# Hybrid decoder trunk: twelve unit pairs a layer by seven products, weight sums built in scratch memory by accumulating transfers

## The chip, the cores and the metric

One core of one Trainium2 chip runs the whole program. The metric is device time in microseconds (us) of one execution, the median of several. A profiled execution gives the trace that is read below; the trace's span runs from the first instruction to the last, and the execution's own time is a little longer than its span.

The core has a matrix engine (PE in the profile, with its weight loads as PEld), a vector engine (DVE), a scalar engine (ACT), a general engine (POOL), and a queue that issues transfers (SP). POOL can issue transfers too. Each engine works through its own list of instructions in order and waits at an instruction until what it needs is there.

## The reference, cut to what matters

Two layers, each on 512 tokens of width 1024:

```
h    = rmsnorm(x) ; proj = h @ w_in            # q,k,v,z,b,a | q,k,v | gate A, gate B
y_a  = deltanet(...) @ w_up_dn                 # gated delta rule, 8 heads of 128
y_b  = sliding_window_attention(...) @ w_up_sw # 16 query heads, window 128
mix  = (sigmoid(gA) * y_a + sigmoid(gB) * y_b) @ w_o
x    = x + rmsnorm(mix)
ff   = square(relu(rmsnorm(x) @ w_ff1)) @ w_ff2   # 1024 -> 4096 -> 1024
x    = x + rmsnorm(ff)
```

Everything is float32. The kernel keeps that precision by splitting each operand into a rounded part and a remainder and by summing three products (high x high, high x low, low x high), so one product of two blocks is three matmuls.

## The kernel before, in words

**Weights.** All weight chunks lie packed in one input, `wpk`, 128 partitions by 1024 numbers each (512 KB). `load` brings one chunk into a buffer `wr` (six of them, `WR`); `prefetch` rounds it on ACT into `wh` (line 384) and takes the remainder on DVE into `wl` (line 385); `weights()` hands out the next chunk and keeps four split chunks ahead (`LOOK`). The list `specs` fixes the order of chunks for the whole program, and each of its entries is a chunk to load or a small function that makes one.

**A layer in order.** The B projections; then the attention loop of 16 rounds, in which each round computes one or more input-projection units (`MIX`: K for DeltaNet keys, G and A for gates) and one group of sliding-window attention (`att_group`); then branch B's up projection (eight `ps_us` units); then the DeltaNet heads; then branch A's up projection (`ps_ud`), the output projection (`ps_wo`) and the MLP.

In a round of the attention loop the second half of a group masks the transposed probabilities on POOL (two selects `pc`, line 1017, one for the rounded part and one for the remainder) and PE multiplies them with the values (`ps_o`, line 1023). POOL also computes the powers `irk` (line 829) and the rotary products `rt` (lines 911 to 916). SP moves each head's decay matrix `D`, keys `kkd` and matrix `ud` to and from scratch memory; DVE uses `D` at line 837.

**The MLP.** The hidden width of 4096 is cut into four groups `s` of eight units of 128 columns. A single unit is `mm_a`: 8 blocks of the contraction times three matmuls, each 128 by 128 by 512 columns. Two neighbouring units may instead be computed together, as a 2 by 2 block product by seven half-size products (a Strassen-Winograd form): `ff1` calls `mm_h` seven times, each 4 blocks times three matmuls of 256 columns. The operands of these products on the side of the weights are sums of the two units' halves; those on the side of the tokens (`n1` to `n4`) are made once a layer by `combos`. `SEQ` says which units of a group go singly and which as a pair; before the change group 0 has only singles, group 1 two pairs, group 2 three, group 3 four: nine pairs a layer.

The sums of a pair's weights are made by `up_specs`/`one`: it loads both units into two `wr` buffers and adds their halves on DVE into two more (line 343, four additions of 128 by 512 a pair). A pair then uses three and a half chunks: the first unit, sum a, sum b, and the second half of the second unit.

Groups 0 to 2 multiply the result with `w_ff2` by seven products again (`mm_c`: P1 to P7, two chunks each, 24 matmuls of 512 columns a product). Their left operands are made by `lefts` after every second pair (or fourth unit), P1 among them. The last product of a group, P4 (`fourth`), is split in two and its second half put into the next group's first pair when that group begins with a pair.

**What sets the order.** The code is traced in program order, then a scheduler with a model of durations places each instruction in its engine's list. Where the code opens an `Order`, the traced order of the named engines is kept; `keep_in_program_order` pins a single instruction. A transfer issued by SP waits in SP's list until the buffers it needs are free, and everything behind it in that list waits with it.

Of the kernel before, what the change touches and what calls it, by code (L numbers as in the profile page):

```python
# [20 lines left out]
P = 128  # L21
# [20 lines left out]
WR = 6  # L42
FF_ORDER = (0, 4, 1, 5, 2, 6, 3, 7)
XB = 6
SEQ = (FF_ORDER, (0, 1, (4, 5), (2, 3), 6, 7), ((0, 1), (4, 5), (2, 3), 6, 7), ((0, 1), (2, 3), (4, 5), (6, 7)))
# [82 lines left out]
def hybrid_trunk(ctx, tc, x, positions, pre_mix_g, dn_conv_w, dn_a_log, dn_dt_bias, dn_norm_g,  # L128
# [193 lines left out]
    def up_specs(l, s):  # L322
# [4 lines left out]
        def unit(m):  # L327
            return load(("w_ff1", l, 0, (s * 8 + m) * P, 0))

        def one(ms):  # L330
            b = {}

            def raw():
                b["0"], b["1"] = (unit(m) for m in ms)
                return b["0"]

            def of(n_):
                b[n_] = wp.tile([P, 1024], F32, name="wr", bufs=WR)
                x0, x1, x2, x3 = b["0"][:, :512], b["0"][:, 512:], b["1"][:, :512], b["1"][:, 512:]
                yb = b["a"][:, 512:]  # L340
                for o_, i0, i1 in (((b[n_][:, :512], x0, x2), (yb, b[n_][:, :512], x3)) if n_ == "a" else
                                   ((b[n_][:, 512:], x2, x3), (b[n_][:, :512], yb, x1))):
                    tt(out=o_, in0=i0, in1=i1, op=ALU.add)  # L343
                return b[n_]

            return raw, lambda: of("a"), lambda: of("b"), lambda: b["1"][:, 512:]
# [13 lines left out]
        return out + [(last, -1)] * bool(last)  # L360

# [243 lines left out]
    for l in range(depth):  # L605
# [437 lines left out]
        late, klate = (), []  # L1043
        for i in range(16):
            us = []
# [249 lines left out]
        for m in range(KT):  # L1295
# [5 lines left out]
            steps(2 if m < 6 else 40)  # L1301
            if m == 1:
                turn0()
# [66 lines left out]
        mm_b4(pss, mT)  # L1370
        m0, s0 = [], []
# [93 lines left out]
        def ff1(done, rest=None):  # L1465
# [4 lines left out]
            for n, e in enumerate(SEQ[s]):  # L1470
                if not isinstance(e, tuple):
# [35 lines left out]
                mm_h(y, c2, 4, ops["n2"], False)  # L1507
# [5 lines left out]
                mm_h(z, c2, 0, ops["n1"], False)  # L1513
# [18 lines left out]
        for s in range(3):  # L1532
# [9 lines left out]
            def lefts(X, Y):  # L1542

                a11, a21, a12, a22 = X[:, 0:512], X[:, 512:1024], Y[:, 0:512], Y[:, 512:1024]
                make("P1", T[5], a11)
# [17 lines left out]
            def done(ms, ps):  # L1563
# [130 lines left out]
```

## Time and profile before

| | us |
|---|---|
| median of 3 runs (1818.12 to 1818.74) | 1818.7 |
| the profiled execution's own time | 1816.19 |
| its span | 1814.5 |
| PE busy in the span | 1794.6 |
| DVE busy | 1375.1 |
| ACT busy | 1007.5 |
| POOL busy | 210.6 |

The granted TensorE clock was 0.999 over the span. The transfer engines were busy for 49.2% of the span with SP's queue and 0.0% with POOL's.

How to read it: a group of instructions is given as line, engine, operation, output<-input, shapes, count, busy time and mean duration in ns. A matmul's duration is longer than the distance to the next one, since matmuls are pipelined; what a matmul costs PE is the distance between starts, which the rows in order of time show. In those rows the first column is the start in us from the span's start, the second the duration in us, and a bracket at the end tells how long the engine had been idle and what released it. `x2` at the end of a row means two such instructions, merged.

### The profile page before, as it was taken

Reading aid. Unit: us, or ns where it says so; the run is one execution under the profiler, and the core shown is the slowest. Engines: PE = TensorE matmul, PEld = TensorE weight load, DVE = VectorE, ACT = ScalarE, POOL = GpSimd, SP = SyncE. Lnnn points to the kernel's source line nnn. Section 1 sums busy time; section 2 is a strip of 40 time slices with the busy share of each in tenths; the row PEclk is TensorE's granted clock in tenths of the full one; section 3 lists DMA queues with packets and bytes.
Section 4 is the critical chain, followed back from the end, with each engine's and each line's share of the span. In section 5 each row is a group of like instructions: output and inputs, shape, how many; then the busy total and the mean of one; then the engine's idle time right before and its main releaser. Section 6 shows DMA issues by size and latency. Waiting matters only on the chain.

```text
span 1814.5 us, 28394 instructions
## 1 busy us (share of the span) xinstructions
PE 1794.6 (99%) x10252; PEld 1524.7 (84%) x10252; DVE 1375.1 (76%) x2590; ACT 1007.5 (56%) x2065; POOL 210.6 (12%) x386
## 2 busy tenths in 40 slices
PE   9999999999999999999999999999999999999998
PEld 8878878888788888989898887888877888889896
DVE  5499796887666878898556997968875669698973
ACT  6678742444434656566556877234443347566572
POOL 0322102221101000000013221022111010000000
PEclk9999999999999999999999999999999999999999
DMA  5633447655463254554445334585545533555551
GB/s 201 203 112 121 111 146 226 178 172 152 117 208 129 82 164 156 174 180 145 168 160 176 106 127 111 169 232 159 163 140 154 171 116 105 174 162 164 174 178 56
DMA packets 146431, 278.60 MB, mean 154 GB/s; under 512 B 33569, under 2 KB 66657, under 8 KB 146290
## 3 DMA queue, kind: packets, MB, share of 16 engines
q1 hardware_dynamic: 145778, 276.75, 49.2%
q8 instruction: 81, 1.33, 0.3%
q14 instruction: 60, 0.49, 0.1%
q0 software_dynamic: 512, 0.03, 0.0%
HBM read 239.38 MB, written 37.36 MB: 153 GB/s over the span
## 4 chain that ended last, share of the span: by engine, by line
PE 88%; DVE 4%; ACT 4%; DMA 2%; issue 1%; POOL 0%; SPq 0%; DVEq 0%; POOLq 0%; ACTq 0%
PE ps_b L459 3%; PE ps_b L461 3%; PE ps_b L463 3%; PE ps_f L400 2%; PE ps_f L401 2%; PE ps_f L402 2%; PE ps_us L400 2%; PE ps_ud L400 2%; PE ps_us L401 2%; PE ps_ud L401 2%; PE ps_ud L402 2%; PE ps_us L402 2%; PE ps_vp L400 2%; PE ps_vp L402 2%; PE ps_vp L401 1%; PE ps_qp L401 1%
## 5 line engine op out<-in xcount | busy, mean ns | idle before, releaser
L384 ACT CAST wh<-wr 128x1024 fp32r<-128x1024 f32 (+2 forms) x368 | 372.7, 1019 | 430.4 <-PE ps_us L401 60.2
L385 DVE TENSOR_TENSOR wl<-wr,wh 128x1024 fp32r<-128x1024 f32 (+2 forms) x368 | 434.9, 1189 | 183.8 <-ACT wh L384 180.2
L526 POOL TENSOR_TENSOR pr<-pq,pw 128x1 f32<-128x1 f32 x16 | 9.8, 615 | 790.1 <-DVE pq L525 790.1
L459 PE MATMUL ps_b<-wh,h_h 128*128 128x432 f32 (+1 forms) x192 | 71.1, 370 | 0.0
L461 PE MATMUL ps_b<-wl,h_h 128*128 128x432 f32 (+1 forms) x192 | 70.4, 367 | 0.0
L463 PE MATMUL ps_b<-wh,h_l 128*128 128x432 f32 (+1 forms) x192 | 70.3, 366 | 0.0
L400 PE MATMUL ps_f<-g_h,wh 128*128 128x512 f32 x160 | 62.4, 390 | 0.0
L401 PE MATMUL ps_f<-g_l,wh 128*128 128x512 f32 x160 | 62.4, 390 | 0.0
L402 PE MATMUL ps_f<-g_h,wl 128*128 128x512 f32 x160 | 62.2, 389 | 0.0
L401 PE MATMUL ps_qp<-h_l,wh 128*128 128x512 f32 x128 | 53.9, 421 | 0.0
L400 PE MATMUL ps_vp<-h_h,wh 128*128 128x512 f32 x128 | 53.7, 420 | 0.0
L402 PE MATMUL ps_vp<-h_h,wl 128*128 128x512 f32 x128 | 53.7, 419 | 0.0
L995 ACT ACTIVATE M<-M,nm 128x128 f32<-128x128 f32 x128 | 49.8, 391 | 5.9 <-DVE nm L990 5.8
L400 PE MATMUL ps_qp<-h_h,wh 128*128 128x512 f32 x128 | 51.8, 405 | 0.0
L343 DVE TENSOR_TENSOR wr<-wr 128x512 f32<-128x512 f32 x72 | 47.5, 685 | 5.5 <-DMA wr<-in_weights_dram 5.2
L400 PE MATMUL ps_kp<-h_h,wh 128*128 128x512 f32 x128 | 51.6, 403 | 0.0
L402 PE MATMUL ps_qp<-h_h,wl 128*128 128x512 f32 x128 | 51.4, 401 | 0.0
L401 PE MATMUL ps_vp<-h_l,wh 128*128 128x512 f32 x128 | 51.3, 401 | 0.0
L401 PE MATMUL ps_ga<-h_l,wh 128*128 128x512 f32 x128 | 51.0, 398 | 0.0
L400 PE MATMUL ps_gb<-h_h,wh 128*128 128x512 f32 x128 | 51.0, 398 | 0.0
L402 PE MATMUL ps_kp<-h_h,wl 128*128 128x512 f32 x128 | 50.9, 398 | 0.0
L402 PE MATMUL ps_ga<-h_h,wl 128*128 128x512 f32 x128 | 50.7, 396 | 0.0
(435 smaller groups left out, 5928.4 us busy)
## 6 DMA issues: line engine op xcount, KB each, us to landing
wr<-in_weights_dram SPq DMA_DIRECT2D x320, 512.0 KB, 3.6
wr<-in_weights_dram SPq DMA_DIRECT2D x24, 432.0 KB, 5.2
D<-dd SPq DMA_DIRECT2D x32, 256.0 KB, 2.7
xd<-xo SPq DMA_DIRECT2D x12, 512.0 KB, 3.0
xt<-xd SPq DMA_DIRECT2D x24, 256.0 KB, 4.5
D<-gd SPq DMA_DIRECT2D x16, 256.0 KB, 6.2
dd<-D SPq DMA_DIRECT2D x16, 256.0 KB, 5.2
kkd<-kk SPq DMA_DIRECT2D x16, 256.0 KB, 2.0
```

Of the source, the lines that this page charges most:

```text
L343: tt(out=o_, in0=i0, in1=i1, op=ALU.add)
L384: nc.scalar.copy(wh[:, :w], wr[:, :w])
L385: sub(out=wl[:, :w], in0=wr[:, :w], in1=wh[:, :w].bitcast(F32), op=ALU.subtract)
L400: mm(ps, lhsT=wh[:, k, :], rhs=hi, start=k == 0, stop=False)
L401: mm(ps, lhsT=wh[:, k, :], rhs=lo, start=False, stop=False)
L402: mm(ps, lhsT=wl[:, k, :], rhs=hi, start=False, stop=k == KT - 1)
L459: mm(pss[t], lhsT=hi[:, tsl], rhs=wh[:, r, :], start=k == 0 and not onto, stop=False, skip_group_check=onto)
L461: mm(pss[t], lhsT=hi[:, tsl], rhs=wl[:, r, :], start=False, stop=False, skip_group_check=onto)
L463: mm(pss[t], lhsT=lo[:, tsl], rhs=wh[:, r, :], start=False, stop=k == KT - 1, skip_group_check=onto)
L526: ptt(out=r, in0=q1, in1=mhalf[:, 0:1], op=ALU.pow)
L995: act(out=M[:, j * P:(j + 1) * P], in_=M[:, j * P:(j + 1) * P], func=AF.Exp, bias=nm[:, j:j + 1], accum_out=den[:, j:j + 1])
```

## The change

It does five things.

1. `SEQ` now pairs all units of groups 1, 2 and 3: four pairs each, twelve a layer. Six pairs are new in the program (three a layer).
2. The weight sums are no longer made on DVE. For each pair and layer there is a scratch tile `fs` (128 by 2048 numbers) in device memory. A generator `prepare` fills it in four stages: two plain transfers issued by SP copy both units into it (256 rows of 512 numbers each); then three transfers issued by POOL add onto it in place: 256 rows, then 128 rows, then 128 rows of 512 numbers. Each stage of a pair is one call after the stage before.
3. `next(ready)` makes one call. At a call the oldest pair's last stage, the next pair's third, the next one's second and the newest pair's first are issued together: two SP transfers and three POOL transfers in a full call. There are 15 calls a layer: seven in the attention loop, two in branch B's up projection, one after the first half of the output projection, and five in the MLP.
4. A pair's chunks are then loads: the first unit, two halves of `fs`, and the second half of the second unit. The order in which a pair uses the two halves of the second sum is swapped to fit.
5. P1's left operand is made after the first pair of two instead of in `lefts`, and in groups 1 and 2 the accumulators of the products `pa` and `py` change places between two sets of PSUM buffers.

```diff
-SEQ = (FF_ORDER, (0, 1, (4, 5), (2, 3), 6, 7), ((0, 1), (4, 5), (2, 3), 6, 7), ((0, 1), (2, 3), (4, 5), (6, 7)))
+FF_PAIRS = ((0, 1), (4, 5), (2, 3), (6, 7))
+SEQ = (FF_ORDER, FF_PAIRS, FF_PAIRS, ((0, 1), (2, 3), (4, 5), (6, 7)))
...
         def one(ms):
-            b = {}
-
-            def raw():
-                b["0"], b["1"] = (unit(m) for m in ms)
-                return b["0"]
-
-            def of(n_):
-                b[n_] = wp.tile([P, 1024], F32, name="wr", bufs=WR)
...
-                    tt(out=o_, in0=i0, in1=i1, op=ALU.add)
-                return b[n_]
-
-            return raw, lambda: of("a"), lambda: of("b"), lambda: b["1"][:, 512:]
+            d = sums[l, s, ms]
+
+            def of(c, w=1024):
+                wr = wp.tile([P, 1024], F32, name="wr", bufs=WR)
+                dma(wr[:, :w], d[:, c * 1024:c * 1024 + w])
+                return wr
+
+            def tail():
+                wr = wp.tile([P, 1024], F32, name="wr", bufs=WR)
+                dma(wr[:, :512], wpk[index["w_ff1", l, 0, (s * 8 + ms[1]) * P, 0], :, 512:])
+                return wr
+
+            return lambda: unit(ms[0]), lambda: of(0), lambda: of(1), tail
...
+    pairs = [(s_, e) for s_, seq in enumerate(SEQ) for e in seq if isinstance(e, tuple)]
+    sums = {(l, *p): dr.tile([P, 2048], F32, name=f"fs{l}{p[0]}{p[1][0]}")
+            for l in range(depth) for p in pairs}
+
+    def prepare(l):
+        here = tc.keep_in_program_order
+
+        def stages(s_, e):
+            i = index["w_ff1", l, 0, (s_ * 8 + e[0]) * P, 0]
...
+            v = sums[l, s_, e][:, :].rearrange("p (h t c) -> p h t c", h=2, t=2)
+            for t in range(2):
+                here(dma(v[:, :, t, :], wpk[i + t].rearrange("p (h c) -> p h c", h=2)))
+            yield
+            here(pdma(v[:, :, 1, :], wpk[i:i + 2, :, 0:512].rearrange("t p c -> p t c"),
+                      accum_op=ALU.add))
+            yield
+            here(pdma(v[:, 0, 0, :], v[:, 1, 1, :], accum_op=ALU.add))
+            yield
+            here(pdma(v[:, 1, 0, :], v[:, 0, 0, :], accum_op=ALU.add))
+
+        todo = [stages(*p) for p in pairs]
+        for n in range(len(todo) + 3):
+            for g in todo[max(n - 3, 0):n + 1]:
+                next(g, None)
+            yield
...
+        ready = prepare(l)
         for i in range(16):
+            if i in (0, 2, 4, 6, 8, 11, 14):
+                next(ready)
...
             steps(2 if m < 6 else 40)
+            if m in (1, 4):
+                next(ready)
...
         mm_b4(pss, mT)
+        next(ready)
...
             for n, e in enumerate(SEQ[s]):
+                if (s, n) == (1, 1):
+                    next(ready)
...
-                mm_h(y, c2, 4, ops["n2"], False)
+                mm_h(y, c2, 0, ops["n2"], False)
...
-                mm_h(z, c2, 0, ops["n1"], False)
+                mm_h(z, c2, 4, ops["n1"], False)
...
-                make("P1", T[5], a11)
...
                 count[0] += len(ms)
+                if ms[-1] in (1, 3):
+                    make("P1", T[5], raw[0][:, 0:512])
...
+                    if s == 0 and i in (1, 5):
+                        next(ready)
...
-            pa = [PZ("ps_pa") for t in range(2)]
+            pa = [(PM if s else PZ)("ps_pa") for t in range(2)]
             mm_c(pa, left["P1"])
-            py = [PM("ps_py") for t in range(2)]
+            py = [(PZ if s else PM)("ps_py") for t in range(2)]
...
             make_later("P2", T[5])
+            if s < 2:
+                next(ready)
```

PE's list in the attention loop is the same before and after; it differs only in the MLP and by two neighbouring swaps in the DeltaNet heads. The transfers enter POOL's and SP's lists, and ACT's list changes in the MLP. Three places follow. After the change the lines are shifted (1017 is 1044, 829 is 856, 816 is 843, 384 is 411, and so on).

POOL in the first layer's attention loop, before; the end of one group's selects, the power of a key head, and the selects of the groups after it:

```order
L1017 AFFINE_SELECT pc<-pf_l 128x512
L829 TENSOR_TENSOR irk<-ssk,pw 128x4
L1017 AFFINE_SELECT pc<-pf_h 128x512
L1017 AFFINE_SELECT pc<-pf_l 128x512
L1017 AFFINE_SELECT pc<-pf_h 128x512
L1017 AFFINE_SELECT pc<-pf_l 128x512
L1017 AFFINE_SELECT pc<-pf_h 128x512
L829 TENSOR_TENSOR irk<-ssk,pw 128x4
```

The same place after the change (lines 381, 379 and 376 are the fourth, third and second stage of a pair):

```order
L1044 AFFINE_SELECT pc<-pf_l 128x512
L381 DMA fs_112<-fs_112 128x512
L379 DMA fs_113<-fs_113 128x512
L376 DMA fs_114<-in_weights_dram 256x1x512
L856 TENSOR_TENSOR irk<-ssk,pw 128x4
L1044 AFFINE_SELECT pc<-pf_h 128x512
L1044 AFFINE_SELECT pc<-pf_l 128x512
L1044 AFFINE_SELECT pc<-pf_h 128x512
L1044 AFFINE_SELECT pc<-pf_l 128x512
L381 DMA fs_113<-fs_113 128x512
L379 DMA fs_114<-fs_114 128x512
L376 DMA fs_115<-in_weights_dram 256x1x512
```

Three transfers now stand between a group's last select and the next instruction; these are the third and the fourth call of the layer.

SP in the same loop, before, from a key head's store on:

```order
L813 DMA kkd<-kk 128x512
L816 DMA D<-dd 128x512
L282 DMA wr<-in_weights_dram 128x1024
L813 DMA kkd<-kk 128x512
L839 DMA ud<-uu 128x4x128
```

The same place after:

```order
L840 DMA kkd<-kk 128x512
L374 DMA fs_113<-in_weights_dram 256x512 x2
L843 DMA D<-dd 128x512
L283 DMA wr<-in_weights_dram 128x1024
L840 DMA kkd<-kk 128x512
```

The two copies of a pair's first stage go ahead of the load of the next decay matrix.

ACT in group 1 of the first layer's MLP, where its last unit gives way to P1 (1571 and 1572 are a single unit's relu and square, 1516 to 1525 a pair's, 497 and 500 the splits of the left operands, 1593 the copy for `py`), before:

```order
L384 CAST wh<-wr 128x1024
L1571 ACTIVATE raw<-ps_f_7522 128x2x256
L1572 ACTIVATE raw<-raw 128x2x256
L497 ACTIVATE P_h<-raw 128x512
L500 CAST P_h<-raw 128x512
L500 CAST P_h<-S_7560 128x512
L384 CAST wh<-wr 128x1024
L500 CAST P_h<-S_7561 128x512
L1593 ACTIVATE ps_py<-ps_pa 128x512 x2
```

The same place after:

```order
L411 CAST wh<-wr 128x1024
L1559 ACTIVATE raw<-ps_z 128x256
L1557 ACTIVATE raw<-raw 128x512
L1560 ACTIVATE raw<-raw 128x1024
L411 CAST wh<-wr 128x1024
L524 ACTIVATE P_h<-raw 128x512
L527 CAST P_h<-S_7751 128x512
L411 CAST wh<-wr 128x1024
L1631 ACTIVATE ps_py<-ps_pa 128x512 x2
```

Where a single unit's two instructions stood, a pair's three stand now, before the same splits.

More of the change, by code (lines that the diff above doesn't have):

```diff
@@ L330, in one @@
         def one(ms):
-            b = {}
-            def raw():
-                b["0"], b["1"] = (unit(m) for m in ms)
-                return b["0"]
-            def of(n_):
-                b[n_] = wp.tile([P, 1024], F32, name="wr", bufs=WR)
[L339 to L343, printed above, removed]
-                return b[n_]
-            return raw, lambda: of("a"), lambda: of("b"), lambda: b["1"][:, 512:]
+            d = sums[l, s, ms]
[8 more added lines that the diff above has]
+            return lambda: unit(ms[0]), lambda: of(0), lambda: of(1), tail
         last = None
@@ L360, in up_specs @@
         return out + [(last, -1)] * bool(last)
+    pairs = [(s_, e) for s_, seq in enumerate(SEQ) for e in seq if isinstance(e, tuple)]
[5 more added lines that the diff above has]
+            i = index["w_ff1", l, 0, (s_ * 8 + e[0]) * P, 0]
+            assert index["w_ff1", l, 0, (s_ * 8 + e[1]) * P, 0] == i + 1
+            v = sums[l, s_, e][:, :].rearrange("p (h t c) -> p h t c", h=2, t=2)
[13 more added lines that the diff above has]
+            yield
     specs = []
```

## The prediction

> **What bounds the kernel now.** I read the page first, then the groups by line, the busy times of chosen stretches, and PE, POOL, SP and ACT in order of time where the change touches them.
>
> ```profile
> span 1814.5 us, 28394 instructions
> PE 1794.6 (99%) x10252; PEld 1524.7 (84%) x10252; DVE 1375.1 (76%) x2590; ACT 1007.5 (56%) x2065; POOL 210.6 (12%) x386
> PE 88%; DVE 4%; ACT 4%; DMA 2%; issue 1%; POOL 0%; SPq 0%; DVEq 0%; POOLq 0%; ACTq 0%
> ```
>
> PE is busy for all but 19.9 us of the span, and the chain of waits lies on it for 88%. So a change helps if it takes matmuls away, and hurts if it makes PE wait. The stages differ in how close PE is to waiting (MLP of the first layer, its group 3, attention loop):
>
> ```profile
> 620.00:900.00 280.00, 280.00 (x1593) 247.10 (x1592) 225.88 (x281) 172.42 (x270) 1.62 (x3) 1.00 0.50 162
> 823.00:863.00 40.00, 40.00 (x325) 39.55 (x324) 31.48 (x44) 30.54 (x55) 0.00 (x0) 1.00 0.48 157
> 100.00:240.00 140.00, 138.27 (x707) 111.71 (x706) 121.54 (x365) 111.85 (x336) 33.24 (x57) 1.00 0.37 111
> ```
>
> The columns are length, then busy time of PE, PEld, DVE, ACT and POOL, clock, transfer engines' share and GB/s. In the MLP PE never waits, though DVE is 81% busy: the sums on DVE are hidden, and taking them away gives nothing back there. In the attention loop PE waits for 1.7 us in 140: there everything is close.
>
> **The change part by part: the matmuls.** Six pairs of single units become six pairs by seven products. Two single units are 2 x 8 x 3 = 48 matmuls of 512 columns; a pair is 7 x 4 x 3 = 84 of 256.
>
> ```profile
> L400 PE MATMUL ps_f<-g_h,wh 128*128 128x512 f32 x160 | 62.4, 390 | 0.0
> L487 PE MATMUL ps_z<-n_h,wh 128*128 128x256 f32 x144 | 41.0, 285 | 0.0
> ...
> 667.78 0.39 PE L401 MATMUL ps_f<-g_l,wh 128*128 128x512 f32 x1
> ...
> 672.31 0.28 PE L487 MATMUL ps_a<-g_h,wh 128*128 128x256 f32 x1
> ...
> 673.75 0.40 PE L400 MATMUL ps_f<-g_h,wh 128*128 128x512 f32 x1
> ```
>
> The durations (390 and 285 ns) overlap and would say that a pair gets dearer: 48 x 390 = 18.7 us against 84 x 285 = 23.9. The starts decide. From 667.78 to 672.31 stand 20 matmuls of 512 columns, 226.5 ns each; from there to 673.75 twelve of 256, 120 ns each. A pair costs 84 x 0.120 = 10.08 us against 48 x 0.2265 = 10.87: 0.79 less. Six pairs: **-4.75 us**. The saving is not the full eighth because half the columns cost more than half the time.
>
> **The sums on DVE** (nothing on the path).
>
> ```profile
> L343 DVE TENSOR_TENSOR wr<-wr 128x512 f32<-128x512 f32 x72 | 47.5, 685 | 5.5 <-DMA wr<-in_weights_dram 5.2
> ```
>
> These 47.5 us go, but PE waited for none of them in the MLP. The new pairs bring ACT and DVE more splits and evictions; group 3 already runs four pairs in a row with them at 76% and 79% and PE never idle. I count zero. The first pair of group 1 now follows group 0 at once; its last token operand, `n4`, is used only by the pair's last product, some 10 us in. Zero too.
>
> **The calls on POOL.** 72 accumulating transfers are issued by POOL. The trace has one transfer of POOL's, of 128 rows of 16 bytes:
>
> ```profile
> L1216 POOL DMA_DIRECT2D fd<-ff x16: 590/620/757, 348.9 to 1393.3; - x16
> ```
>
> A full call issues 256 + 128 + 128 rows. If an issue has a fixed cost, the call takes 3 x 0.59 = 1.8 us; if it goes by rows, 4 x 0.62 = 2.5; if the destination must be read and so counts again, 8 x 0.62 = 5.0. I take 2.5, since a row should cost alike. What waits behind a call in the attention loop are the selects, and PE waits for those:
>
> ```profile
> 129.91 0.64 POOL L1017 TENSOR_SCALAR_AFFINE_SELECT pc<-pf_l 128x512 fp32r<-128x512 f32 x1 [1.46 <-DVE es L992]
> 133.68 1.91 POOL L829 TENSOR_TENSOR irk<-ssk,pw 128x4 f32<-128x4 f32 x1 [3.13 <-DVE ssk L827]
> 135.56 0.63 POOL L1017 TENSOR_SCALAR_AFFINE_SELECT pc<-pf_h 128x512 fp32r<-128x512 f32 x1
> 137.81 0.63 POOL L1017 TENSOR_SCALAR_AFFINE_SELECT pc<-pf_l 128x512 fp32r<-128x512 f32 x1 [1.63 <-DVE nm L990]
> ...
> 145.74 0.64 POOL L1017 TENSOR_SCALAR_AFFINE_SELECT pc<-pf_l 128x512 fp32r<-128x512 f32 x1 [0.68 <-DVE es L992]
> 151.56 0.64 POOL L1017 TENSOR_SCALAR_AFFINE_SELECT pc<-pf_h 128x512 fp32r<-128x512 f32 x1 [5.18 <-ACT pf_h L500]
> 152.29 1.01 POOL L829 TENSOR_TENSOR irk<-ssk,pw 128x4 f32<-128x4 f32 x1
> 153.68 0.47 POOL L912 TENSOR_TENSOR rt<-qt,cs 128x128 f32<-128x128 f32 x1
> 154.42 0.63 POOL L1017 TENSOR_SCALAR_AFFINE_SELECT pc<-pf_l 128x512 fp32r<-128x512 f32 x1 [0.27 <-DVE pf_l L501]
> ...
> 138.93 0.63 PE L1023 MATMUL ps_o<-pc,vp 128*128 128x512 f32 x2
> 154.97 0.63 PE L1023 MATMUL ps_o<-pc,vp 128*128 128x512 f32 x2
> ...
> PEld ps_o L1023 <- POOL pc L1017: 2.1, 7, 0.6
> 180.94 1.01 POOL L829 TENSOR_TENSOR irk<-ssk,pw 128x4 f32<-128x4 f32 x1 [6.92 <-DVE ssk L827]
> 213.56 0.64 POOL L1017 TENSOR_SCALAR_AFFINE_SELECT pc<-pf_h 128x512 fp32r<-128x512 f32 x1 [8.61 <-ACT pf_h L500]
> ```
>
> The third call stands behind the select that ends at 130.55. After it come `irk` (1.91) and two selects (0.63 each), and PE's second `ps_o` starts 0.23 after 138.93: 139.16 - 130.55 - 3.17 = 5.4 us of room. The fourth stands at 146.38: select, `irk`, two rotary products (0.47 each) and the next select are 3.2 us, and PE needs the last at 155.20: 5.6 us of room. So calls of 1.8 to 5.0 us fit: **0 us**; each us beyond 5.4 costs a us at both places, in both layers. The fifth and sixth stand in gaps of 6.92 and 8.61 us, the first two ahead of rotary products that a later block of tokens uses, and in the MLP POOL has nothing else to do.
>
> **The transfers.** A call adds two copies and three additions, 2 MB in all, to transfer engines that are half idle.
>
> ```profile
> q1 hardware_dynamic: 145778, 276.75, 49.2%
> wr<-in_weights_dram SPq DMA_DIRECT2D x320, 512.0 KB, 3.6
> D<-dd SPq DMA_DIRECT2D x32, 256.0 KB, 2.7
> SPq L282 <- DVE wl L385: 643.5, 203, 12.9
> 175.51 0.42 SPq L816 DMA_DIRECT2D D<-dd  x1
> 189.66 0.35 DVE L837 SCALAR_TENSOR_TENSOR uu<-ps_a,cj,D 128x128 f32<-128x128 f32 x1
> ```
>
> The additions of a call, one after another at the rate of these loads, are 3.6 + 2.7 + 2.7 = 9.0 us; twice that, 18.0, if reading the destination doubles them. The next call's additions wait on POOL for them; the nearest two calls are 130.55 and 146.38, 15.8 us apart, and the room of 5.6 less 2.5 for issuing comes on top: POOL is late only beyond 18.9 us. I take 9.0. The copies go ahead of a decay matrix `D` in SP's list: two issues (0.42 each) and 2 x 3.6 = 7.2 us at most if nothing overlaps, 8.0 in all. `D` is issued at 175.51 and first used at 189.66, which leaves 14.2 - 2.7 = 11.5. Weight loads wait for free buffers (643.5 us of SP's time), so they run ahead and bear a delay. **0 us**; were that cover gone, 8.0 us a call would be the most.
>
> **The handover to P1** in groups 1 and 2. A pair's last evictions are longer than a unit's.
>
> ```profile
> 706.13 0.39 PE L475 MATMUL ps_pa<-wh,P_h 128*128 128x512 f32 x1
> 706.11 1.05 ACT L384 CAST wh<-wr 128x1024 fp32r<-128x1024 f32 x1 [2.99 <-PE ps_f L401]
> 709.40 0.62 ACT L500 CAST P_h<-S 128x512 fp32r<-128x512 f32 x1
> 710.23 0.69 DVE L501 TENSOR_TENSOR P_l<-S,P_h 128x512 fp32r<-128x512 f32 x1
> ```
>
> P5's second operand is ready at 710.9, 4.8 us after the last unit; PE wants it after P1 and half of P5, 36 x 0.2265 = 8.15 us. A pair adds at most about 1.5 us (a square and a relu over twice the columns). **0 us**, with 1.8 us to spare.
>
> **The sum**: -4.75 us against the profiled execution's span of 1814.5 (its own time 1816.19, 2.5 us under the median): a span of 1809.75. Put on the median of the runs: 1818.7 - 4.75 = **1814.0 us**.
>
> **The rivals.** *POOL is held up by its transfers* (slower). The trace shows POOL stretched by its neighbours: `irk` takes 1.01 us at 152.29 and 1.91 at 133.68. A call at the upper count, stretched alike, takes 5.0 x 1.9 = 9.5 us: 4.1 late at the third call, 3.9 at the fourth, 16 in two layers: 1818.7 - 4.75 + 16 = 1830. It makes the kernel slower from a call of 7.6 us on. Against it: the sixteen transfers seen differ by only 590 to 757 ns, beside a busy DVE. Chance 0.08; a call of 6 to 7.5 us ends near the old time, 0.06. The Trainium skill ("SBUF — State Buffer", "Who interferes with whom") speaks for this rival: a transfer issued by GpSimd has its descriptors written through a port pair that DVE can lock, and elsewhere it puts such a wait at some 3100 ns for a transfer of 620; by that a call would take 9.3 us. But it ties the lock to copies, casts and scalar operations, and DVE's groups in this loop are mostly additions and products of two tensors.
>
> *The additions are slow.* At 25 us for a call's additions POOL is 25 - 18.9 = 6.1 us late at the fourth call, 12.2 in two layers: 1826. The bound of 18.0 speaks against it. Chance 0.04.
>
> *The handover makes PE wait.* If DVE or ACT has two more chunks to split ahead of P5's operand (2 x 1.05 on ACT and their remainders), PE waits about 1 us at four handovers: 1818, no change to speak of. For it: ACT is 76% busy where four pairs run in a row. Chance 0.15.
>
> *More is won than matmuls*: 5.5 us or more, by stalls that happen to fall better; only 19.9 us of idle time are there at all, little of it near the change. Chance 0.05. Something I don't see: 0.02, half of it slower.
>
> **How the numbers follow.** The forecast has 0.60. A measurement of this kernel tells about 0.2% from no change, 3.6 us, so the line lies at 1815.1 and the forecast clears it by only 1.1 us; I give 0.05 of its 0.60 to "the same". Faster: 0.55 + 0.05 = 0.60. Same: 0.05 + 0.06 + 0.15 + 0.01 = 0.27. Slower: 0.08 + 0.04 + 0.01 = 0.13. The range reaches from 1812.5 (1.5 us won besides) to 1819.5, which takes in the handover and the middle call lengths and leaves out the two slow rivals. The forecast's own range is 1812.5 to 1815.5.
>
> **What would show it.** Right: PE's groups at the single units' line fall by 288 matmuls and those at the three lines of the half-size products rise by 504, still 226.5 and 120 ns apart; PE busy for all of the MLP; `ps_o` starting as close behind `pc` as now; POOL's three new lines below 1.8 us an issue on average; written bytes up by 50 MB. Wrong: idle time of PE put down to `pc`, to `D`, to `P_h`, or to a load from `fs`; POOL's new lines at 2.5 us and more.

## The result: 12.5 us slower, and where they came from

The changed kernel takes 1831.2 us (median of four runs, 1828.8 to 1833.9) against 1818.7 (1818.1 to 1820.1) for the kernel before on the same chip: ratio 1.0068, 95% interval 1.0050 to 1.0085. The forecast was 1814.0 with a range to 1819.5.

The page of the kernel after: span, engines, traffic, the chain of waits, a group of matmuls that had no idle time ahead of it before, and the new transfers (size and time to landing).

```profile
span 1832.2 us, 29147 instructions
PE 1797.1 (98%) x10468; PEld 1532.6 (84%) x10468; DVE 1353.2 (74%) x2542; ACT 1024.3 (56%) x2101; POOL 277.4 (15%) x458
HBM read 308.58 MB, written 87.69 MB: 216 GB/s over the span
PE 81%; DVE 7%; DMA 4%; ACT 4%; issue 2%; SPq 1%; POOL 1%; DVEq 0%; POOLq 0%; ACTq 0%
L428 PE MATMUL ps_ud<-yT_l,wh 128*128 128x512 f32 x128 | 51.6, 403 | 8.3 <-DVE yT_l L528 8.3
fs<-in_weights_dram SPq DMA_DIRECT2D x48, 512.0 KB, 5.5
fs<-in_weights_dram POOLq DMA_DIRECT2D x24, 512.0 KB, 9.6
fs<-fs POOLq DMA_DIRECT2D x48, 256.0 KB, 6.8
```

PE is idle for 35.1 us instead of 19.9, though it has 216 matmuls more and 4.75 us less to do. The chain leaves PE for DVE, ACT and transfers for 7%, 4% and 4% of the span. To see where, I cut both traces at the same matmuls and took the distance between their starts: attention loop from the first `ps_pt` to the first `ps_us`; branch B's up part and DeltaNet from there to the first `ps_ud`; branch A and output projection to the last transpose (`ps_n`) ahead of the MLP; MLP to the next layer's last `ps_n` or the last matmul.

| us | attention 1, 2 | branch B, DeltaNet 1, 2 | branch A, w_o 1, 2 | MLP 1, 2 |
|---|---|---|---|---|
| before | 157.6, 157.6 | 243.6, 245.4 | 99.7, 99.7 | 332.0, 318.2 |
| after | 159.8, 161.2 | 244.4, 245.1 | 105.2, 106.3 | 331.5, 316.9 |

From the unrounded starts that is +5.8, +0.6, +12.2 and -1.8, with 0.9 ahead of the first layer's attention loop: the 17.7 us between the two spans. (The profiled execution of after is the slowest of its four, that of before 2.5 under its median; by the medians the loss is 12.5.) Three places, in the order of their size:

**Branch A waits for the last tail.** The last DeltaNet head's normalisation goes through memory: POOL writes 2 KB (`fd<-ff`), SP reads it back to all partitions (`fb<-fd`), DVE multiplies (`yf`). This way through memory is called the bounce below. POOL, SP and DVE in order of time, first before, then after, and PE's matmul that waits:

```profile
494.49 0.59 POOL L1216 DMA_DIRECT2D fd<-ff  x1 [0.29 <-POOL ff L1215]
497.85 0.32 SPq L1219 DMA_DIRECT2D fb<-fd  x1
502.75 0.69 DVE L1220 TENSOR_TENSOR yf<-yf,fb 128x512 f32<-128x512 f32 x1 [7.43 <-DMA fb<-fd]
```

```profile
498.83 0.61 POOL L1246 DMA_DIRECT2D fd<-ff  x1 [0.30 <-POOL ff L1245]
499.45 0.94 POOL L381 DMA_DIRECT2D fs<-fs  x1
500.03 1.21 POOL L379 DMA_DIRECT2D fs<-fs  x1
500.57 1.74 POOL L376 DMA_DIRECT2D fs<-in_weights_dram  x1
504.94 0.32 SPq L1249 DMA_DIRECT2D fb<-fd  x1
512.65 0.69 DVE L1250 TENSOR_TENSOR yf<-yf,fb 128x512 f32<-128x512 f32 x1 [12.70 <-DMA fb<-fd]
514.30 0.50 PE L428 MATMUL ps_ud<-yT_l,wh 128*128 128x512 f32 x1 [3.54 <-DVE yT_l L528]
```

From `fd` to `yf` it took 8.3 us; now 13.8. In between POOL issues a whole call, 1 MB of additions: the call stands in the program behind the output projection's first products (`ps_b`), which PE runs from 543 to 565 us, 44 to 65 us later, but POOL had nothing to wait for and went ahead. The second layer has the same, 9.3 against 15.6 us, and PE waits 4.28.

**A DVE instruction in the attention loop takes 2.1 us instead of 0.3.** DVE before, DVE after, and PE after:

```profile
155.50 0.78 DVE L501 TENSOR_TENSOR vp<-kv,vp 128x128 fp32r<-128x128 f32 x2
```

```profile
156.83 2.33 DVE L528 TENSOR_TENSOR vp<-kv,vp 128x128 fp32r<-128x128 f32 x2 [0.84 <-ACT vp L527]
158.60 0.21 POOL L943 TENSOR_TENSOR kv<-rt 128x16 f32<-128x16 f32 x1
161.00 0.36 PE L1004 MATMUL ps_s<-kT_h,qT 128*128 128x256 f32 x1 [1.90 <-DVE M L1012]
```

Of the row's two instructions the first has 2.13 us. POOL's rotary products run without a break through all of it; the last ends at 158.81, DVE's instruction at 158.96. The same, to 10 ns, happens in the second layer.

**The MLP** gains 0.5 and 1.3 us instead of 2.4 a layer. After the last pair of a group DVE has the operands of the next products and the sums of their weights to make, and PE waits for a weight that ACT rounds late, because DVE summed it late (PE, ACT, DVE after; group 1 of the first layer, then of the second):

```profile
739.49 0.73 PE L502 MATMUL ps_pw<-wh,P_h 128*128 128x512 f32 x2 [0.47 <-ACT wh L411]
738.38 1.99 ACT L411 CAST wh<-wr 128x1024 fp32r<-128x1024 f32 x2 [3.38 <-DVE wr L310]
736.79 1.23 DVE L310 TENSOR_TENSOR wr<-wr 128x1024 f32<-128x1024 f32 x1 [0.45 <-DMA wr<-in_weights_dram]
1648.46 0.73 PE L502 MATMUL ps_pv<-wh,P_h 128*128 128x512 f32 x2
1646.41 2.00 ACT L411 CAST wh<-wr 128x1024 fp32r<-128x1024 f32 x2 [2.57 <-DVE wr L310]
1645.10 1.22 DVE L310 TENSOR_TENSOR wr<-wr 128x1024 f32<-128x1024 f32 x1
```

In the first layer the sum itself started 0.45 us late because its load had not landed; in the second DVE had no pause ahead of it. In the MLP of the kernel before no matmul starts more than 0.1 us later than the usual 226.5 or 120 ns after the one ahead of it. In the kernel after such late starts are found only in the last pair and the products of groups 1 and 2, and add up to 1.8 and 1.0 us in the two layers, most of it where P7 (`ps_pw`) takes its second weight chunk and P3 (`ps_pv`) its first, some 25 us after the handover to P1. These waits are called the handover's below.

**The clock adds to the waits.** Three stretches of the kernel after (length, busy times, granted clock, share of the transfer engines, GB/s):

```profile
515.10:518.40 3.30, 3.30 (x9) 2.59 (x8) 2.14 (x3) 1.09 (x2) 0.00 (x0) 0.50 0.82 316
1068.10:1071.40 3.30, 3.30 (x9) 2.54 (x8) 3.30 (x19) 1.99 (x10) 1.02 (x1) 0.50 0.07 22
1423.10:1426.30 3.20, 2.88 (x7) 2.30 (x8) 1.20 (x3) 0.79 (x2) 0.00 (x0) 0.50 0.71 271
```

After each wait of PE of 3.5 and 4.3 us, and after one of the two of 1.9, TensorE ran at half its clock for 3.41 us, which costs 1.7 us: 5.1 of the 17.7. Before, PE never paused that long between its first and last matmuls, and no such stretch is there. The Trainium skill ("TensorE: Matmul & The Clock Gate", "What's actually happening") says that the clock falls to half after an idle window of about 3.4 us and comes back after a busy one. The length of the stretches agrees; that a wait of 1.9 us can bring one on does not.

### The profile page after: what moved, and what is told of

It is laid out like the page before. It is cut to its first block, busy times and chain, and to the rows that moved or that the text cites. A ratio compares the mean times of both kernels' runs of the same rounds, so it can differ in the third digit from the quotient of the medians.

```text
span 1832.2 us, 29147 instructions
## 1 busy us (share of the span) xinstructions
PE 1797.1 (98%) x10468; PEld 1532.6 (84%) x10468; DVE 1353.2 (74%) x2542; ACT 1024.3 (56%) x2101; POOL 277.4 (15%) x458
## 4 chain that ended last, share of the span: by engine, by line
PE 81%; DVE 7%; DMA 4%; ACT 4%; issue 2%; SPq 1%; POOL 1%; DVEq 0%; POOLq 0%; ACTq 0%
PE ps_b L486 3%; PE ps_b L488 3%; PE ps_b L490 3%; PE ps_us L427 2%; PE ps_us L429 2%; PE ps_us L428 2%; PE ps_vp L427 2%; PE ps_vp L429 2%; PE ps_vp L428 1%; PE ps_qp L428 1%; PE ps_qp L427 1%; PE ps_qp L429 1%; PE ps_z L514 1%; PE ps_a L517 1%; PE ps_a L516 1%
## 5 line engine op out<-in xcount | busy, mean ns | idle before, releaser
L411 ACT CAST wh<-wr 128x1024 fp32r<-128x1024 f32 (+2 forms) x380 | 381.5, 1013 | 415.2 <-PE ps_us L428 55.9
L412 DVE TENSOR_TENSOR wl<-wr,wh 128x1024 fp32r<-128x1024 f32 (+2 forms) x380 | 446.2, 1184 | 195.4 <-ACT wh L411 190.8
L428 PE MATMUL ps_ud<-yT_l,wh 128*128 128x512 f32 x128 | 51.6, 403 | 8.3 <-DVE yT_l L528 8.3
L514 PE MATMUL ps_z<-n_h,wh 128*128 128x256 f32 x192 | 54.9, 286 | 0.0
L517 PE MATMUL ps_a<-g_h,wl 128*128 128x256 f32 x192 | 54.3, 283 | 0.0
L516 PE MATMUL ps_a<-g_l,wh 128*128 128x256 f32 x192 | 54.3, 283 | 0.0
L517 PE MATMUL ps_z<-n_h,wl 128*128 128x256 f32 x192 | 54.3, 283 | 0.0
L516 PE MATMUL ps_z<-n_l,wh 128*128 128x256 f32 x192 | 54.3, 283 | 0.0
L514 PE MATMUL ps_a<-g_h,wh 128*128 128x256 f32 x192 | 54.3, 283 | 0.0
```

Source lines behind the costliest of these rows:

```text
L411: nc.scalar.copy(wh[:, :w], wr[:, :w])
L412: sub(out=wl[:, :w], in0=wr[:, :w], in1=wh[:, :w].bitcast(F32), op=ALU.subtract)
L428: mm(ps, lhsT=wh[:, k, :], rhs=lo, start=False, stop=False)
L514: mm(ps, lhsT=wh[:, k0 + k, :], rhs=hi, start=start and k == 0, stop=False, skip_group_check=True)
L516: mm(ps, lhsT=wh[:, k0 + k, :], rhs=lo, start=False, stop=False, skip_group_check=True)
L517: mm(ps, lhsT=wl[:, k0 + k, :], rhs=hi, start=False, stop=k == 3, skip_group_check=True)
```

## The experiments

Each run is compared with runs of the kernel before on its own chip, where the medians of before were 1817.5 to 1821.3. Stages are cut as above, "+" is against the kernel before's trace; the stage of branch B and DeltaNet moves by 2 to 3 us between traces with the same instructions there, and so small a difference in it isn't read. Branch A too is 1.6 to 2.0 us longer in one of the two layers of e1_dve_sums, e11_eight, e12_dve_ten and e13_four, which have no call there (two of them have no additions at all): PE waits 1.4 to 1.7 us for the head before the last, whose bounce takes 10.2 to 10.5 us in them and 7.8 to 7.9 in the trace of before, which has no such wait.

| run | us | ratio, 95% interval |
|---|---|---|
| e1_dve_sums | 1824.8 | 1.0020, 1.0009 to 1.0032 |
| e2_old_units | 1835.4 | 1.0080, 1.0062 to 1.0097 |
| e3_late_ninth | 1821.7 | 1.0005, 0.9996 to 1.0014 |
| e4_thin | 1819.7 | 0.9994, 0.9984 to 1.0005 |
| e5_moved | 1857.6 | 1.0221, 1.0205 to 1.0236 |
| e6_fd_sp | 1823.8 | 1.0036, 1.0022 to 1.0050 |
| e7_ten | 1861.8 | 1.0246, 1.0230 to 1.0261 |
| e8_spread | 1846.1 | 1.0128, 1.0107 to 1.0148 |
| e10_nudge | 1820.6 | 0.9995, 0.9987 to 1.0004 |
| e11_eight | 1820.2 | 0.9995, 0.9987 to 1.0004 |
| e12_dve_ten | 1819.2 | 0.9990, 0.9981 to 0.9998 |
| e13_four | 1817.1 | 0.9983, 0.9974 to 0.9992 |

### The sums without the pairs, the pairs without the transfers

```diff
-            d = sums[l, s, ms]        # loads of the sums from fs
+            b = {}                    # as before: both units loaded, sums added by DVE
...
-        ready = prepare(l)
+        ready = iter(lambda: 0, 1)    # calls do nothing
```

> Twelve pairs a layer as in the changed kernel, but the weight sums are added by DVE as in the kernel before; no transfers to scratch memory at all. Theory: the changed kernel's 12.5 us are three losses and one gain. Losses worked out from the offsets of the two traces: some 11 us where branch A waits for the last tail (3.7 and 5.4 us in one gap each), some 5.6 us in the attention loop (a gap of 2.06 us in each layer), some 3.1 us at handovers of the MLP (idle before ps_pw and ps_pv); gain 4.75 us of matmuls. Then only the handovers remain: 1818.7 - 4.75 + 3.1 = 1817.0. Rival: the pairs themselves cost the time (handovers, evictions): 1825 to 1831.

Measured: 1824.8, 3.9 above the kernel before on its chip. Attention is back (-0.1, 0.0), but the MLP is 3.5 and 3.7 us longer, not 1 shorter: twelve pairs' sums are too much for DVE behind a handover. PE waits for the first sums of the next group:

```profile
749.09 0.39 PE L520 MATMUL ps_y<-n_h,wl 128*128 128x256 f32 x1 [0.92 <-DVE wl L415]
```

The time lies between the two, just short of the rival's range. The theory had the handovers' price right for sums that come by transfer only; with DVE making them the pairs cost more than they bring. Against the changed kernel's MLP this one is 4.0 and 5.1 us longer, so the transfers do buy something.

```diff
-SEQ = (FF_ORDER, FF_PAIRS, FF_PAIRS, ((0, 1), (2, 3), (4, 5), (6, 7)))
+SEQ = (FF_ORDER, (0, 1, (4, 5), (2, 3), 6, 7), ((0, 1), (4, 5), (2, 3), 6, 7), ((0, 1), (2, 3), (4, 5), (6, 7)))
```

> The unit order of the kernel before (nine pairs, six single units more), but the sums of the nine pairs are built in scratch memory as in the changed kernel; twelve calls do work, the tenth among them. Theory: no matmul gain, no handover loss, the losses at branch A and in the attention loop stay: 1818.7 + 11 + 5.6 = 1835. Rival (the pairs cost the time): 1819.

Measured: 1835.4, 14.5 above before. The MLP is within 0.2 us of before in both layers, with PE never idle at a handover, though nine pairs load their sums from memory; attention (+2.0, +2.3) and branch A (+6.8, +5.2) carry the loss. The pairs are not the cause of it.

### The call behind the last tail

```diff
         mm_b4(pss, mT)
-        next(ready)
...
-                    if s == 0 and i in (1, 5):
+                    if s == 0 and i in (1, 3, 5):
                         next(ready)
```

> The changed kernel with one call of each layer moved: the one that POOL issues right behind the last tail's fd transfer, 40 us ahead of its place in the program, comes after the first statistics of the output projection instead (it is called from group 0's fourth unit). Theory (the call's 1 MB of additions share transfer engines with the 2 KB bounce fd, fb that the yT split waits for): the gaps before ps_ud vanish, 1831.2 - 10 = 1821. Rival (scratch traffic slows everything wherever it stands): 1830 to 1832, with the gaps before ps_ud still there.

Measured: 1821.7, 0.05% above before where the changed kernel is 0.68% above it. The call is the layer's tenth. Branch A is back at 0.0 and +0.9 us, `fd` to `yf` at 8.2 and 9.1 us (POOL and DVE, first layer):

```profile
500.85 0.61 POOL L1246 DMA_DIRECT2D fd<-ff  x1 [0.30 <-POOL ff L1245]
509.07 0.69 DVE L1250 TENSOR_TENSOR yf<-yf,fb 128x512 f32<-128x512 f32 x1 [7.17 <-DMA fb<-fd]
```

The attention loop keeps its loss (+3.6, +2.1), with one half-clock stretch, now in the first layer. The additions are not slower than the kernel can bear; one call stood in the wrong place.

```diff
-            here(pdma(v[:, :, 1, :], wpk[i:i + 2, :, 0:512].rearrange("t p c -> p t c"),
+            here(pdma(v[:, :, 1, :16], wpk[i:i + 2, :, 0:16].rearrange("t p c -> p t c"),
...                                   # and [:16] in the other two additions
```

> The changed kernel whose additions move 16 columns of each row instead of 512, so that most of each sum is left out: same copies, same rows, same instructions on POOL, a thirty-second of the bytes. Theory: what makes the tail late is the bytes, so the gaps before ps_ud vanish; the gap in the attention loop comes from the order of POOL's and DVE's work and may stay: 1820 to 1822. Rival (issuing on POOL costs the time): 1830 to 1832.

Measured: 1819.7. POOL's issues take as long as in the changed kernel (the last of a call 1.74 us in both), but the bounce takes 9.4 and 9.7 us instead of 13.8 and 15.6, and branch A is at 0.0 and +0.5 us. So it is the bytes in flight that delay the bounce, not POOL's time (POOL and DVE, first layer):

```profile
499.22 1.74 POOL L376 DMA_DIRECT2D fs<-in_weights_dram  x1
506.90 0.69 DVE L1250 TENSOR_TENSOR yf<-yf,fb 128x512 f32<-128x512 f32 x1 [8.45 <-DMA fb<-fd]
```

```diff
-            pdma(fd[h, :].rearrange("(p j) -> p j", p=P), ff)
+            dma(fd[h, :].rearrange("(p j) -> p j", p=P), ff)
```

> The changed kernel, whose 2 KB transfers fd go through SP's queue instead of POOL's; the call behind the last tail stays where it is. Theory (the additions slow the bounce by using the same transfer engines and memory, whatever queue it is in): the gaps before ps_ud stay for the most part, 1827 to 1832. Rival (fd is late because it shares POOL's queue with the additions): the gaps vanish, 1821.

Measured: 1823.8, 6.2 above before: between the two. The trace decides (second layer, SP and DVE):

```profile
1397.16 0.32 SPq L1246 DMA_DIRECT2D fd<-ff  x1
1399.00 0.38 SPq L1249 DMA_DIRECT2D fb<-fd  x1
1410.45 0.69 DVE L1250 TENSOR_TENSOR yf<-yf,fb 128x512 f32<-128x512 f32 x1 [13.58 <-DMA fb<-fd]
```

`fb` now follows `fd` after 1.8 us instead of 6.3, but `fb`, which always went by SP, then takes 11.5 us instead of 9.3 (4.7 before the change). The whole bounce is 13.3 us in this layer and 13.4 in the first. Another queue hardly helps; what is shared lies behind the queues. The Trainium skill ("DMA: Bandwidth & Descriptors", "Queues, rings and completion order") says that each transfer engine takes turns between the queues it has work for, a packet at a time, which fits; whether the engines or the memory behind them are what is shared is not shown. The time came down by half all the same because of the first layer: there `fd` leaves 3.2 us after the first `ps_ud` instead of 5.0, so that PE waits 1.32 us instead of 3.54 and keeps its clock, and the DVE instruction in attention happened to get through. In the second layer branch A is at +7.2.

### The DVE instruction and POOL's rotary products

```diff
-            if i in (0, 2, 4, 6, 8, 11, 14):
+            if i in (0, 2, 11, 14):
...
             d_chain(h)
+            if h in (1, 3):
+                next(ready)
...                                   # late ninth as above; (1, 3) added to (1, 1) in ff1
```

> The changed kernel with five calls of each layer moved: the one behind the last tail (as in e3_late_ninth) and, in the attention loop, the calls at the units 4, 6 and 8, so that between 105 and 175 us POOL issues nothing; they stand in the DeltaNet loop (two) and in the MLP instead. Theory (the 2.06 us gap before ps_s comes from a DVE instruction, vp<-kv,vp, that takes 2.1 instead of 0.3 us while POOL runs its rotary products without a break, and the calls only shift the two against each other): the instruction is back at 0.3 to 0.6 us and the gap away; what is left is the gain of 4.75 us less the handovers' 3.1 us, 1.2 to 1.7 us under the kernel before. Rival (something else in the change brings the gap): 1 us above the kernel before, with the gap.

Measured: 1857.6, 40 above before. In the attention loop it went as the theory said: the instruction takes 0.55 and 0.33 us, and attention is at +0.1 and 0.0. But the two calls that went to the DeltaNet loop cost 20.9 and 18.7 us there. DVE works through its list in order, and a head's `yf` waits in it for its bounce, ahead of a copy that PE needs at once (DVE and PE, first layer):

```profile
387.66 0.69 DVE L1250 TENSOR_TENSOR yf<-yf,fb 128x512 f32<-128x512 f32 x1 [8.34 <-DMA fb<-fd]
388.27 0.28 DVE L1302 COPY St<-ps_su 128x128 f32<-128x128 f32 x1
388.60 0.80 PE L1288 MATMUL ps_ks<-St,kk 128*128 128x128 f32 x2 [7.88 <-DVE St L1302]
```

The same run with ten pairs (groups 1 and 2 end with two single units) tests the handover:

```diff
+SEQ = (FF_ORDER, FF_PAIRS[:3] + (6, 7), FF_PAIRS[:3] + (6, 7), ((0, 1), (2, 3), (4, 5), (6, 7)))
```

> As e5_moved, but groups 1 and 2 end with two single units instead of a fourth pair: ten pairs a layer, four fewer than in the changed kernel in both layers together, one more a layer than before. Theory (the handover losses come from the pair at the end of a group, whose evictions put DVE behind): no idle of PE before ps_pv and ps_pw; gain 2 x 0.79 = 1.6 us, no loss, so 1.6 us under the kernel before and level with e5_moved. Rival (the losses come from the loads of the sums): PE still idle there, 0.5 us or more above e5_moved's time.

Measured: 1861.8; the DeltaNet loss covers the time, so only the stages speak. PE has no wait at a handover, and the MLP is 0.5 us shorter in each layer, for one pair more than before (0.79 forecast). Against e5_moved, whose MLP is at +0.5 and -1.0 with waits of 0.3 to 0.9 us at `ps_pw` and `ps_pv`, that bears the theory out; the times of the two tell nothing on it.

```diff
                 ...                   # e3_late_ninth, and in att_rope:
+                if t == 3 and nh == QH:
+                    ptt(out=tm[0][:, 0:2], in0=x1[:, 0:2], in1=cb[:, 0:2], op=ALU.mult)
                 ptt(out=tm[0], in0=x1, in1=cb, op=ALU.mult)
```

> As e3_late_ninth, with one small product more on POOL (16 columns, some 0.2 us) ahead of the rotary products of the fourth block of tokens; the calls of the attention loop stay where the change put them. Theory (the gap before ps_s is a matter of phase: the DVE instruction is shut out for 2.1 us when it comes 0.39 us into POOL's fourth product, and gets in when it comes 0.2 us into one): the instruction is back at 0.3 to 0.6 us, the gap is away in both layers, 4 us less than e3_late_ninth, 1.2 to 1.7 us under the kernel before. Rival (the calls hold the attention loop up by themselves): the gap stays, 1 us above the kernel before.

Measured: 1820.6 (0.9995), half of what was expected. DVE's instruction now comes 0.22 us into POOL's product in both layers; in the first it takes 0.38 us and PE waits 0.15 at `ps_s`, in the second it takes 2.16 and PE waits 1.77. In e4_thin and e6_fd_sp it comes 0.39 to 0.40 us into the product in both layers, and again takes 0.38 us in the first and 2.00 and 2.10 in the second. So the moment alone does not decide. Over all the traces: where calls stand between 105 and 150 us (and at the same place of the second layer) the instruction was shut out 9 times of 12, where none stand there 0 times of 16. That the calls there bring the wait on is shown. That POOL's unbroken run is what holds the instruction up rests on the times (all nine end within 0.15 us of that run's end); no run takes the products away, and what decides who gets in stays open.

### Other places for the calls

```diff
-            if i in (0, 2, 4, 6, 8, 11, 14):
+            if i in (0, 2, 11, 13, 15):
...
-            if m in (1, 4):
+            if m in (1, 3, 5):
...                                   # the other seven in the MLP
```

> The changed kernel with its calls placed by what the runs so far showed: none in the attention loop between 105 and 175 us (units 0, 2, 11, 13, 15), three in branch B's up part, none in the DeltaNet loop, none behind the last tail, the other seven in the MLP. Theory (losses: ninth call some 10 us, phase of POOL against DVE 4.1 us, handovers 3.1 us; gain 4.75 us): only the handovers stay, 1.2 to 1.7 us under the kernel before. Rival (seven calls in the MLP slow its weight loads): PE idle in group 0 and 1, some us above the kernel before.

Measured: 1846.1, 25 above. Attention is at +0.3 and 0.0, but three calls in branch B's up part cost 16.2 and 7.5 us by the next stage's bounce, and the MLP with its seven is 2.9 and 2.7 us longer, as the rival had it (the longest wait, 2.0 us, stands at the products of group 0). DVE's list again, where the first row was 3.5 us in the kernel before:

```profile
DVE Pc L920 <- DMA Tc<-pd: 28.0, 2, 16.5
DVE yf L1250 <- DMA fb<-fd: 25.7, 10, 7.5
```

So the calls have few places to go, and fewer calls were tried next. Two kernels keep the calls at the units 0, 2, 11 and 14 and the two in branch B, put the rest (five and one) into the MLP, and sum the other pairs on DVE:

```diff
     pairs = [(s_, e) for s_, seq in enumerate(SEQ) for e in seq if isinstance(e, tuple)
+             and s_ < 3]                                              # e11_eight
+             and (s_, e[0]) in ((1, 6), (2, 0), (2, 6), (3, 0))]      # e13_four
```

> Twelve pairs a layer, the sums of groups 1 and 2 (eight pairs) in scratch memory, those of group 3 on DVE as in the kernel before; the eleven calls stand at units 0, 2, 11 and 14 of the attention loop, two in branch B's up part, five in group 0 and the start of group 1; none in the DeltaNet loop and none behind the last tail. Theory (every call is free where neither a bounce through memory nor POOL's rotary products stand next to it): gain 4.75 less handovers 2 to 3 us, 1.7 to 2.7 us under the kernel before (ratio 0.9985 to 0.999). Rival (the calls in group 0 slow its weight loads as in e8_spread): PE idle in the first layer's group 0, level with the kernel before or above.

Measured: 1820.2, level with before. That is the rival's time, but not its cause: PE has no late start in group 0. The MLP is at +1.0 and -0.2, with waits for group 3's first DVE sums (0.9 and 1.1 us) as in e1_dve_sums.

> Twelve pairs a layer, only four of them with sums in scratch memory (the last pair of groups 1 and 2 and the first of groups 2 and 3, where DVE is behind after a handover), the other eight summed on DVE; seven calls a layer, at units 0, 2, 11 and 14 of the attention loop, two in branch B's up part and one in group 0. Theory: as e11_eight but hardly any scratch traffic in the MLP: 1.7 to 3 us under the kernel before. Rival (DVE's backlog is the same wherever the sums are, as in e1_dve_sums): 2 to 4 us above.

Measured: 1817.1 against 1820.7, ratio 0.9983 with an interval below 1: some 3 us under the kernel before, and faster than the changed one too (1.0068). The MLP is at -1.3 and -1.2, attention at 0.0 in both layers, and no stretch between PE's first and last matmuls has half the clock. Attention loop and MLP of this kernel:

```profile
104.00:244.00 140.00, 138.47 (x701) 111.92 (x701) 121.61 (x358) 111.29 (x332) 37.93 (x62) 1.00 0.51 135
628.00:908.00 280.00, 279.71 (x1710) 251.41 (x1709) 230.74 (x291) 182.47 (x292) 2.18 (x4) 1.00 0.55 176
```

The changed kernel has there:

```profile
104.00:244.00 140.00, 135.94 (x691) 109.60 (x691) 120.75 (x356) 110.16 (x335) 45.52 (x71) 1.00 0.73 181
629.50:909.50 280.00, 279.18 (x1705) 250.63 (x1704) 212.76 (x257) 180.90 (x288) 2.45 (x4) 1.00 0.62 198
```

The verdict rests on the medians. The profiled execution is 2.2 us above its own, its span 3.0 above that of before: the MLP's 2.5 us are won, but the first layer's DeltaNet stage is at +3.5 and the second layer's branch A at +2.0, stages that differ by 2 us and more between other traces too. So four pairs' transfers, where DVE is behind, are worth having. What the other eight cost is not separated: e11_eight has more calls in the MLP, and also makes one of the four on DVE.

```diff
...                                   # sums on DVE, no calls, as in e1_dve_sums
-SEQ = (FF_ORDER, FF_PAIRS, FF_PAIRS, ((0, 1), (2, 3), (4, 5), (6, 7)))
+SEQ = (FF_ORDER, FF_PAIRS[:3] + (6, 7), FF_PAIRS[:3] + (6, 7), ((0, 1), (2, 3), (4, 5), (6, 7)))
```

> Ten pairs a layer, all sums on DVE, no scratch memory, no calls: against the kernel before only units 4 to 7 of group 1 change (one pair more a layer), with the changed kernel's order inside a pair and at the handover. Theory: the pair's gain, 2 x 0.79 = 1.6 us, and no handover loss because each group still ends with single units: ratio 0.999. Rival (a pair more on DVE puts group 1 behind, as in e1_dve_sums): 1 us above the kernel before or more.

Measured: 1819.2 (0.9990), as forecast and just told apart from before. Its one profile does not show where: the MLP is at -0.1 and +0.4 us. I count it as a hint, not as proof of 0.79 us a pair.

## Why the prediction was wrong, step by step

**The matmuls: right.** Counts rose and fell as said (216 more), and in the kernel after twelve matmuls of 256 columns still take 1.44 us, 120 ns each. In e13_four, with the handovers still in the way, 2.5 of the 4.75 us arrived.

**The sums on DVE: right for nine pairs only.** "I count zero" held in that PE was not waiting for the nine pairs' sums. For twelve, e1_dve_sums put a price of 9.0 us on them (its MLP against the changed kernel's, +4.0 and +5.1). The change could not have had its matmuls without taking some sums off DVE.

**The calls on POOL: 2.5 us taken, 2.9 measured** (from the first issue's start at 499.45 to the last one's end at 502.31), inside the bounds, and under the room of 5.4. No issue took more than 1.74 us, so the rival of a POOL held up by its own transfers did not come. The three groups on POOL, with the waits ahead of them:

```profile
L376 POOL DMA_DIRECT2D fs<-in_weights_dram x24 | 35.5, 1481 | 16.8 <-DMA fs<-in_weights_dram 16.8
L379 POOL DMA_DIRECT2D fs<-fs x24 | 24.2, 1007 | 22.5 <-DMA fs<-in_weights_dram 19.7 <-issue 2.8
L381 POOL DMA_DIRECT2D fs<-fs x24 | 20.5, 855 | 48.8 <-DMA fs<-fs 48.8
```

PE's matmuls waited 0.7 us for POOL's selects over the whole program, against 0.6 before. What the step missed is the other direction: it asked whether POOL comes late to PE, not whether POOL keeps DVE out. The row of `irk` stretched from 1.01 to 1.91 us was quoted, and read as POOL's loss alone. The prediction also took only half of what the Trainium skill's section ("SBUF — State Buffer", "Who interferes with whom") says: besides the lock that copies and casts can take, a DVE instruction with two SBUF inputs contends with a POOL instruction that reads SBUF. `vp<-kv,vp` is one, and its 2.13 us fit that; that it was kept out for a whole run of POOL instructions the page does not say.

**The transfers, "0 us": the step that failed.** Each addition lands in 9.6 and 6.8 us, against 9.0 for all three together. That was survivable: POOL's waits for landings (85 us in all) cost PE nothing that can be seen. The mistake was to ask only who waits for the new transfers (the next call) and what stands behind them in SP's list (`D` and the weight loads), and not which other transfers the bytes in flight slow down: small ones that go to memory and back within one stage, for which DVE stops. Their room was 2.0 us at the last tail (bounces 5.6 and 6.3 us longer gave waits of 3.5 and 4.3). The prediction has no rival for it; with the half clock it is 12.2 of the 17.7 us. Nor did it look where the scheduler would put a call that waits for nothing: the call of the last tail ran 44 to 65 us ahead of the products that its line stands behind.

**The handover: a rival at 0.15, and there, at another place.** P5's operand was in time, as worked out. What came late were the sums of the weights of P7 and P3, behind the splits that DVE had to make first. Price: about 1.1 us a layer at the least (2.4 expected, 1.3 won, in e13_four and in the second layer), 1.9 in the first, where a load came late as well; why it did is not shown.

**`n4` and the first pair of group 1, zero: right**; PE has no wait there.

The sum after the fact, in the profiled executions: -4.75 for matmuls, 3.0 at handovers, 5.8 in attention (of it one half-clock stretch, 1.7), 12.2 at branch A (of it two, 3.4), 0.6 in DeltaNet and 0.9 at the start: 17.7. Of these the branch A term is shown by taking it away (e3_late_ninth), the attention term too (e5_moved), and the handover's place by e2_old_units and e7_ten. The last two terms, 1.5 us, have no cause shown and are of the size by which unchanged stages differ.

## What to carry to other kernels

Before adding bulk transfers to engines that look half idle, list every small transfer on the way of a result (write, read back, use) and ask how much room each has: here 1 MB in flight made an 8 us bounce 14 us long. Where an engine works in order, such a bounce stops everything listed behind it, so the same bytes cost nothing in one stage and 10 us a call in another. And a queue's instruction that waits for nothing runs where its engine is free, not where its line stands; look at its place in the order, not in the program.

## What the runs showed of the hardware that was not expected

- A DVE instruction of 0.28 us on two SBUF operands took 2.00 to 2.16 us in nine of twelve chances, ending within 0.15 us of the end of POOL's run of products.
- After or within a PE pause the granted clock could be 0.50 for 3.41 us or a multiple of it (10.24 us in e5_moved, 13.65 in e8_spread). Between PE's first and last matmuls of all the traces, that followed 4 of the 14 pauses of 1.77 to 2.04 us and 18 of the 19 of 2.43 us and more; in e8_spread it also followed two pauses of 0.97 and 0.75 us that stood 1.3 us apart. A stall of 3.5 us thus cost 5.2.
- An accumulating transfer costs POOL 0.85 to 1.0 us to issue for 128 rows and 1.48 for 256, and takes 6.8 us for 256 KB and 9.6 for 512 KB to land. In the same trace a plain copy of 512 KB within device memory took 5.5 us and a plain load of 512 KB 4.1.
